# Two halves of an attention head issued in turn on different rows of the array, in a two-block kernel on one core

## The chip, the cores and the metric

The kernel runs on one core of one Trainium2 chip. The core has five engines with a queue each: TensorE (PE, its weight loads are shown as PEld), VectorE (DVE), ScalarE (ACT), GpSimd (POOL) and SyncE (SP, which here issues nearly all loads). Each of them takes its instructions in the order in which the program puts them. Matmuls write to PSUM, which has eight banks here, and everything else lives in SBUF. The metric is the device time of one execution, in microseconds.

## The reference

Two transformer blocks of width 1024 over 256 tokens, the first with 256 context tokens beside them. Only its attention matters for the change:

```python
def diff_attention(q, k_all, v_all, lam):
    ...
    def one_block(q_blk):
        s = jnp.einsum('bhcqd,bhckd->bhcqk', q_blk, k_all).astype(jnp.float32) * scale
        p = jax.nn.softmax(s, axis=-1)
        a = p[:, :, 0] - lam * p[:, :, 1]
        return jnp.einsum('bhqk,bhkd->bhqd', a.astype(v_all.dtype), v_all)
...
def first_block(x, c, ctx, ...):
    for l in range(DEPTH):                    # DEPTH = 2
        ...
        attn = diff_attn_post(diff_attention(q, k_all, v_all, lam), subln_g[l], lambda_init)
        pool_o = pool_mixer(up, pool_w[l], pool_scale[l])
        conv_o = conformer_conv(ca, cb, conv_dw_w[l], conv_dw_b[l], conv_ln_g[l], conv_ln_b[l])
        mix = jnp.concatenate([attn, pool_o, conv_o], axis=-1)
        x = x + g1 * jnp.einsum('blm,md->bld', mix, w_out[l])
        x = x + g2 * swiglu(...)
        if not last:
            ...                               # the same for the context tokens
```

There are 4 heads (h), and each has two halves (c = 0, 1) of 64 columns of q and k with one common v of 128 columns. The softmax of the second half, times lam, is taken off that of the first.

## The kernel before

All products are fp32 split in a high and a low part (`fp32r`), so that each product is three matmuls: `mm3`, lines L359 (high by high), L360 and L361. Layer 0 runs tokens and context together, 512 rows; layer 1 (the last) has only the 256 tokens as queries, against all 512 keys.

The function `attention` takes a list of units, each one a head j and a tile tt of 128 queries. In layer 0 each call has the units of one head, four calls in all: two units with 256 keys (the context tiles, which see only the context) and two with 512, 16 units altogether. In layer 1 a call has two heads of two units, two calls, 8 units, all with 512 keys. A unit is made by `scores` (two halves one after the other: three matmuls of a 64-row contraction into a bank `ps_sc`, a DVE reduce for the maximum, an ACT `Exp` into tile `e`) and by `values` (DVE joins the halves, L713; four or two transposes, L716; an ACT copy, L718; the matmuls with v, L721; an ACT square and a DVE scaling). The scores of a unit are written one unit ahead of the values of the unit before. `finish` normalizes a head once all its tiles are there (a pow on POOL, L364, and four transposes, L738).

After each unit `each()` puts other work between: eight convolution taps on DVE, some steps of the modulation's product (`fill`: eight steps to a group, each one a load `wmod` of 512 KB with two buffers and four narrow matmuls, L513, whose sums are transposed at the end, L520) and, at fixed units, `pooled(l, j, ...)` for the two groups of pooled channels. `pooled` is a projection of 512 columns (24 matmuls into a bank `ps_mm`), an ACT copy into padded tiles (L767), window sums on POOL (L772 to L781, two sequences) and a small matmul (L782) for each sequence. The conv's norm (`conv_norm`, from L828) follows with sums of one column (L437), a pow and a broadcast matmul (L452), and after it the merges of all parts with `w_out`, whose first product writes `ps_mm_2431` in layer 0.

PSUM in the first block has four pools: `mm` of three banks, `md` of one (the modulation), `sc` of two and `aux` of two. A tile waits until the bank that it gets is read out by its last user.

What sets the order: a scheduler orders the written instructions by a simulated time line of its own; each engine then has one fixed order. `tc.issue_after(P["product"].ins)` holds an instruction behind the newest product.

Of the kernel before, what the change touches and what calls it, by code (L numbers as in the profile page):

```python
# [14 lines left out]
AF = mybir.ActivationFunctionType  # L15
ALU = mybir.AluOpType
AX = mybir.AxisListType
# [260 lines left out]
def tile_two_blocks(ctx: ExitStack, tc: tile.TileContext, w: bass.AP, blk: bass.AP, cols: bass.AP,  # L278
                    rowv: bass.AP, cst: bass.AP, xin: bass.AP, out: bass.AP):
    nc = tc.nc  # L280
    dma, act, dve, pool, pe = nc.sync, nc.scalar, nc.vector, nc.gpsimd, nc.tensor

    P = {"nscr": NSCR, "both": False, "count": 0}
# [74 lines left out]
    def mm3(ps, a, b, start, stop):  # L358
        pe.matmul(ps, a[0], b[0], start=start, stop=False)  # L359
        pe.matmul(ps, a[0], b[1], start=False, stop=False)  # L360
        P["product"] = pe.matmul(ps, a[1], b[0], start=False, stop=stop)  # L361
# [4 lines left out]
    def bank(p):  # L366
        return P[p].tile([128, 512], F32, name="ps_" + p)
# [4 lines left out]
    def st(n=8):  # L372
        return P["wk"].tile([128, n], F32, name=f"st{n}", bufs=8 if n < 64 else 3)
# [313 lines left out]
    def attention(l, h0, qT, kT, v, o, qts, mix, each):  # L687

        lam, sub = coef[l][:2]
        q0 = qts[0]  # L690

        def scores(j, tt):
            nk = 256 if tt < 2 else 512
            mx, s = st(2), st(2)
            e = []
            for c in range(2):
                r = slice(c * 64, c * 64 + 64)
                ps = bank("sc")
                qs = slice((tt - q0) * 128, (tt - q0) * 128 + 128)
                mm3(ps[:, :nk], (qT[j][0][r, qs], qT[j][1][r, qs]), (kT[j][0][r, :nk], kT[j][1][r, :nk]),  # L700
                    True, True)
                dve.tensor_reduce(mx[:, c:c + 1], ps[:, :nk], axis=AX.X, op=ALU.max, negate=True)
                x = P["wk"].tile([128, 512], F32, name="e", bufs=4)
                act.activation(x[:, :nk], ps[:, :nk], AF.Exp, bias=mx[:, c:c + 1], accum_out=s[:, c:c + 1])
                e.append(x)
            return nk, s, e

        def values(j, tt, ss, nk, s, e):
            h = h0 + j
            r, cc = st(2), st(1)  # L710
            dve.reciprocal(r, s)
            dve.scalar_tensor_tensor(cc, s[:, 0:1], r[:, 1:2], lam, op0=ALU.mult, op1=ALU.mult)
            dve.scalar_tensor_tensor(e[0][:, :nk], e[1][:, :nk], cc, e[0][:, :nk], op0=ALU.mult, op1=ALU.add)  # L713
            pt = bank("aux")
            for i in range(nk // 128):
                pe.transpose(pt[:, i * 128:i * 128 + 128], e[0][:, i * 128:i * 128 + 128], ident)  # L716
            aT = P["wk"].tile([128, 512], F32, name="aT", bufs=2)
            act.copy(out=aT[:, :nk], in_=pt[:, :nk])  # L718
            po = bank("aux")
            for i in range(nk // 128):  # L720
                pe.matmul(po[:, :128], aT[:, i * 128:i * 128 + 128], v[i][:, h * 128:h * 128 + 128],  # L721
                          start=(i == 0), stop=(i == nk // 128 - 1))
            q = P["wk"].tile([128, 128], F32, name="sq128")
            i = tt - q0
            act.activation(q, po[:, :128], AF.Square, scale=r[:, 0:1], accum_out=ss[:, i:i + 1])
            dve.tensor_scalar(o[tt][:, h * 128:h * 128 + 128], po[:, :128], r[:, 0:1], None, op0=ALU.mult)

        def finish(j, ss):
            h = h0 + j
            n = len(qts)  # L730
            c = slice(h * 128, h * 128 + 128)
            dve.tensor_scalar(ss[:, :n], ss[:, :n], 1.0 / 128, EPS, op0=ALU.mult, op1=ALU.add)
            rsqrt(ss[:, :n], n)
            for i, tt in enumerate(qts):
                dve.scalar_tensor_tensor(o[tt][:, c], o[tt][:, c], ss[:, i:i + 1], sub, op0=ALU.mult, op1=ALU.mult)
            pt = bank("aux")
            for i, tt in enumerate(qts):
                pe.transpose(pt[:, i * 128:i * 128 + 128], o[tt][:, c], ident)  # L738
            m = slot()
            split(pt[:, :n * 128], m[0][:, :n * 128], m[1][:, :n * 128])  # L740
            mix[h] = m

        units = [(j, tt) for j in range(len(qT)) for tt in qts]
        sums = {j: st(4) for j in range(len(qT))}
        ahead = scores(*units[0])
        for i, (j, tt) in enumerate(units):
            now = ahead
            if i + 1 < len(units):
                ahead = scores(*units[i + 1])
            values(j, tt, sums[j], *now)  # L750
            if tt == qts[-1]:
                finish(j, sums[j])
            each()

    def pooled(l, j, h, seqs, mix):

# [101 lines left out]
    h = new_h()  # L858
# [67 lines left out]
    for l in range(DEPTH):  # L926
# [27 lines left out]
        def each():  # L954
            run_taps(8)
            if not last and unit[0] < len(FILL):
                fill(FILL[unit[0]])
            unit[0] += 1
            if jobs and unit[0] in POOL_AFTER[l]:
                jobs.pop(0)()  # L960
# [227 lines left out]
    r = st(1)  # L1188
# [483 lines left out]
```

## Time and profile before

| what | value |
|---|---|
| median of three runs | 1420.87 us (1414.85 to 1423.79) |
| the profiled execution | 1412.22 us |
| its span (first to last instruction) | 1410.4 us |
| mean granted clock of TensorE | 0.972 |
| TensorE busy | 1340.1 us, 95% |
| DVE busy | 964.5 us, 68% |
| first layer's attention, first score to the end of the last | 118.20 to 220.30 us |
| last layer's first scores | 720.10 us |

The times in views are microseconds from the start of the span. A granted clock of 1.00 is 2.4 GHz, 0.50 is 1.2 GHz. Rows of the timeline name the line of the instruction, its output tile and its inputs; equal instructions that follow each other stand in one row, with an x and their number (a matmul of fp32 type leaves two records).

### The profile page before, as it was taken

What the parts mean: (1) busy time and instruction counts of PE and PEld (TensorE: products, weight loads), DVE (VectorE), ACT (ScalarE), POOL (GpSimd) and SP (SyncE); (2) the same over time, 40 slices, a digit from 0 to 9 for tenths busy, and PEclk for the clock granted to TensorE, in tenths of its full rate; (3) what the DMA queues carried; (4) which work ended last, traced back from release to release, by engine and by line L of the source; (5) the groups of instructions that cost most, each with busy time, mean ns of one, the idle gap of its engine ahead of it and who ended that gap; (6) DMA issues with size and microseconds to landing.
All of it is one profiled execution on the core that took longest, in us unless ns stands there. A gap on an engine that the chain in (4) does not pass through costs nothing. (4 is left out here: it accounts for less than half of the span.)

```text
span 1410.4 us, 22740 instructions
## 1 busy us (share of the span) xinstructions
PE 1340.1 (95%) x8754; PEld 1172.3 (83%) x8754; DVE 964.5 (68%) x1928; ACT 602.9 (43%) x1085; POOL 233.0 (17%) x274
## 2 busy tenths in 40 slices
PE   5999999899999999998988989999999999988999
PEld 2699656798888888888977879999977889878999
DVE  4599755678666767746975755555688676757665
ACT  3333444442213222335344544444565546446443
POOL 0056630220000000014316220000263002000000
PEclk9899988999999999999988999999999999999999
DMA  9424450425445567732321235555664424424554
GB/s 342 170 78 146 156 175 30 137 90 190 160 153 167 187 217 230 240 113 75 108 87 45 95 130 177 189 180 183 191 213 149 142 84 128 150 90 152 192 184 132
DMA packets 61309, 213.53 MB, mean 151 GB/s; under 512 B 6928, under 2 KB 8080, under 8 KB 60944
## 3 DMA queue, kind: packets, MB, share of 16 engines
q1 hardware_dynamic: 60768, 209.91, 45.0%
q10 hardware_dynamic: 432, 2.16, 0.4%
q8 instruction: 69, 1.13, 0.3%
q14 instruction: 40, 0.33, 0.1%
HBM read 211.00 MB, written 1.05 MB: 150 GB/s over the span
## 5 line engine op out<-in xcount | busy, mean ns | idle before, releaser
L349 ACT CAST whi<-wraw 128x1024 fp32r<-128x1024 f32 (+2 forms) x292 | 300.5, 1033 | 528.4 <-PE ps_mm L360 271.5
L350 DVE TENSOR_TENSOR wlo<-wraw,whi 128x1024 fp32r<-128x1024 f32 (+2 forms) x296 | 356.2, 1205 | 173.0 <-ACT whi L349 168.4
L359 PE MATMUL ps_mm<-hH,whi 128*128 128x256 f32 (+1 forms) x1056 | 344.5, 329 | 11.1 <-ACT hH L497 7.5
L360 PE MATMUL ps_mm<-hL,whi 128*128 128x256 f32 (+1 forms) x1056 | 342.9, 326 | 2.5 <-DVE hL L498 2.5
L361 PE MATMUL ps_mm<-hH,wlo 128*128 128x256 f32 (+1 forms) x1056 | 342.3, 326 | 1.3 <-DVE wlo L350 1.3
L359 PEld LDWEIGHTS ps_mm<-hH,whi 128*128 128x128 f32 x1056 | 204.2, 195 | 32.9 <-ACT hH L497 9.3
L360 PEld LDWEIGHTS ps_mm<-hL,whi 128*128 128x128 f32 x1056 | 204.7, 194 | 20.0 <-DVE hL L498 4.1
L361 PEld LDWEIGHTS ps_mm<-hH,wlo 128*128 128x128 f32 x1056 | 204.6, 194 | 17.5 <-DVE wlo L350 2.3
L359 PE MATMUL ps_mm<-hidH,whi 128*128 128x256 f32 (+1 forms) x683 | 214.8, 317 | 2.6 <-ACT hidH L355 1.7
L360 PE MATMUL ps_mm<-hidL,whi 128*128 128x256 f32 (+1 forms) x683 | 214.7, 315 | 0.6 <-DVE hidL L356 0.6
L361 PE MATMUL ps_mm<-hidH,wlo 128*128 128x256 f32 (+1 forms) x683 | 213.8, 315 | 0.0
L360 PE MATMUL ps_mm<-wlo,hH 128*128 128x256 f32 (+2 forms) x464 | 143.9, 312 | 3.2 <-DVE wlo L350 3.2
L361 PE MATMUL ps_mm<-whi,hL 128*128 128x256 f32 (+2 forms) x464 | 142.6, 309 | 0.0
L359 PE MATMUL ps_mm<-whi,hH 128*128 128x256 f32 (+2 forms) x464 | 140.5, 312 | 2.1 <-ACT tm L647 1.4
L359 PEld LDWEIGHTS ps_mm<-hidH,whi 128*128 128x128 f32 x683 | 129.5, 190 | 11.9 <-ACT hidH L355 1.9
L360 PEld LDWEIGHTS ps_mm<-hidL,whi 128*128 128x128 f32 x683 | 129.9, 190 | 9.8 <-DVE hidL L356 1.2
L361 PEld LDWEIGHTS ps_mm<-hidH,wlo 128*128 128x128 f32 x683 | 129.6, 190 | 8.0
L470 POOL TENSOR_TENSOR squares<-squares,scr 128x256 f32<-128x256 f32 (+1 forms) x28 | 31.7, 1131 | 560.2 <-ACT scr L469 559.7
L580 DVE CUSTOM_DVE_ANT_0 ps_md<-wmod,tm 128x512 f32<-128x512 f32 x160 | 111.5, 697 | 10.8 <-DMA wmod<-in_w_dram 8.0
L848 DVE SCALAR_TENSOR_TENSOR xT<-ps_mm,modv,xT 128x256 f32<-128x256 f32 x116 | 52.5, 479 | 73.9 <-PE ps_mm L361 73.9
L364 POOL TENSOR_TENSOR st<-st,mhalf 128x4 f32<-128x4 f32 (+3 forms) x54 | 64.4, 1198 | 200.1 <-DVE st L632 88.1
L360 PEld LDWEIGHTS ps_mm<-wlo,hH 128*128 128x128 f32 x464 | 89.0, 192 | 9.3 <-DVE wlo L350 5.5
(347 smaller groups left out, 1987.2 us busy)
## 6 DMA issues: line engine op xcount, KB each, us to landing
wraw<-in_w_dram SPq DMA_DIRECT2D x271, 512.0 KB, 3.5
wmod<-in_w_dram SPq DMA_DIRECT2D x85, 512.0 KB, 4.2
wraw<-in_w_dram SPq DMA_DIRECT2D x32, 448.0 KB, 3.2
xT<-in_x_dram ACTq DMA_DIRECT2D x2, 1024.0 KB, 7.0
single<-in_w_dram SPq DMA_DIRECT2D x8, 256.0 KB, 7.5
wraw<-in_w_dram SPq DMA_DIRECT2D x4, 288.0 KB, 3.2
tm<-in_rows_dram SPq DMA_DIRECT2D x4, 256.0 KB, 6.1
out_dram<-scr SPq DMA_DIRECT2D x8, 128.0 KB, 1.7
```

The lines of the kernel that those rows point to most:

```text
L349: act.copy(out=hi[:, :m], in_=t[:, :m])
L350: P["split"] = dve.tensor_tensor(lo[:, :m], t[:, :m], hi[:, :m].bitcast(F32), op=ALU.subtract)
L359: pe.matmul(ps, a[0], b[0], start=start, stop=False)
L360: pe.matmul(ps, a[0], b[1], start=False, stop=False)
L361: P["product"] = pe.matmul(ps, a[1], b[0], start=False, stop=stop)
L364: pool.tensor_tensor(t, t, mhalf[:, :n], op=ALU.pow)
L470: eng.tensor_tensor(squares[:, lo:hi], squares[:, lo:hi], q, op=ALU.add)
L580: dve.tensor_tensor_reduce(bank("md"), t[:, i * 512:i * 512 + 512], crow[2 * j + i], 1.0, 0.0, ALU.mult, ALU.add, sums[j][:, i * KD + d:i ...
L848: dve.scalar_tensor_tensor(xT[:, d, r], ps[:, s * 256 - lo:s * 256 - lo + 256], M(l, which, 1 - s)[:, d:d + 1], xT[:, d, r], op0=ALU.mult, ...
```

## The change

Scores are written as six matmuls in turn, one of each half, where the second half's result goes to a bank of `mm` in place of the second bank of `sc`. Each of the six is held behind the one before. The exps are split off into a function of their own, and the first part of `values`, up to the copy of the transposes, becomes `turned`. The loop then runs scores two units ahead and `turned` one unit ahead of `values`; exps of a unit come after the `turned` of the unit two before it.

```diff
         def scores(j, tt):
             nk = 256 if tt < 2 else 512
             mx, s = st(2), st(2)
+            ps = [bank("sc"), bank("mm")]
+            qs = slice((tt - q0) * 128, (tt - q0) * 128 + 128)
+            for i, (a, b) in enumerate(((0, 0), (0, 1), (1, 0))):
+                for c in range(2):
+                    r = slice(c * 64, c * 64 + 64)
+                    with tc.issue_after(P["product"].ins) if i or c else nullcontext():
+                        P["product"] = pe.matmul(ps[c][:, :nk], qT[j][a][r, qs], kT[j][b][r, :nk], start=i == 0,
+                                                 stop=i == 2)
+            for c in range(2):
+                dve.tensor_reduce(mx[:, c:c + 1], ps[c][:, :nk], axis=AX.X, op=ALU.max, negate=True)
+            return nk, ps, mx, s
+
+        def exps(nk, ps, mx, s):
             e = []
             for c in range(2):
-                r = slice(c * 64, c * 64 + 64)
-                ps = bank("sc")
...
-                mm3(ps[:, :nk], (qT[j][0][r, qs], qT[j][1][r, qs]), (kT[j][0][r, :nk], kT[j][1][r, :nk]),
-                    True, True)
-                dve.tensor_reduce(mx[:, c:c + 1], ps[:, :nk], axis=AX.X, op=ALU.max, negate=True)
                 x = P["wk"].tile([128, 512], F32, name="e", bufs=4)
-                act.activation(x[:, :nk], ps[:, :nk], AF.Exp, bias=mx[:, c:c + 1], accum_out=s[:, c:c + 1])
+                act.activation(x[:, :nk], ps[c][:, :nk], AF.Exp, bias=mx[:, c:c + 1], accum_out=s[:, c:c + 1])
...
-        def values(j, tt, ss, nk, s, e):
-            h = h0 + j
+        def turned(j, tt, nk, s, e):
...
             act.copy(out=aT[:, :nk], in_=pt[:, :nk])
+            return nk, r, aT
+
+        def values(j, tt, ss, nk, r, aT):
+            h = h0 + j
             po = bank("aux")
...
-        ahead = scores(*units[0])
-        for i, (j, tt) in enumerate(units):
-            now = ahead
-            if i + 1 < len(units):
-                ahead = scores(*units[i + 1])
-            values(j, tt, sums[j], *now)
-            if tt == qts[-1]:
-                finish(j, sums[j])
-            each()
+        n = len(units)
+        held = {i: exps(*scores(*units[i])) for i in range(min(2, n))}
+        turn = {}
+        for i in range(n + 1):
+            ahead = scores(*units[i + 2]) if i + 2 < n else None
+            if i:
+                j, tt = units[i - 1]
+                values(j, tt, sums[j], *turn.pop(i - 1))
+                if tt == qts[-1]:
+                    finish(j, sums[j])
+            if i < n:
+                turn[i] = turned(*units[i], *held.pop(i))
+                if ahead:
+                    held[i + 2] = exps(*ahead)
+                each()
```

The text grows by 18 lines, so that later lines have other numbers after (L772 becomes L790, L782 L800). In the new order all score matmuls have the one line L702.

TensorE early in layer 0's attention, before: the scores of the first head's second unit and what follows them (`ps_sc` are the scores, `ps_md` the modulation, `ps_mm` a projection).

```order
L359 MATMUL ps_sc_1285<-hidH_670,hidH_661 128x256
L360 MATMUL ps_sc_1285<-hidL_671,hidH_661 128x256
L361 MATMUL ps_sc_1285<-hidH_670,hidL_662 128x256
L359 MATMUL ps_sc_1292<-hidH_670,hidH_661 128x256
L360 MATMUL ps_sc_1292<-hidL_671,hidH_661 128x256
L361 MATMUL ps_sc_1292<-hidH_670,hidL_662 128x256
L513 MATMUL ps_md_1323<-wmod_1324,csil_109 32x256 x4
```

The same place after:

```order
L702 MATMUL ps_mm_1286<-hidH_670,hidH_661 128x256
L702 MATMUL ps_sc_1285<-hidL_671,hidH_661 128x256
L702 MATMUL ps_mm_1286<-hidL_671,hidH_661 128x256
L702 MATMUL ps_sc_1285<-hidH_670,hidL_662 128x256
L702 MATMUL ps_mm_1286<-hidH_670,hidL_662 128x256
L702 MATMUL ps_sc_1301<-hidH_670,hidH_661 128x512
L702 MATMUL ps_mm_1302<-hidH_670,hidH_661 128x512
L702 MATMUL ps_sc_1301<-hidL_671,hidH_661 128x512
```

The halves take turns, and the next unit (512 keys) follows at once.

TensorE at the end of layer 0's attention, after: the last scores, and what comes behind them (`ps_mm_2211` is the first pooled projection, whose products stood, before, between the scores of the first and the second head; the second one, `ps_mm_2289`, and all small pooled matmuls come later still).

```order
L702 MATMUL ps_sc_2173<-hidH_1672,hidL_1664 128x512
L702 MATMUL ps_mm_2174<-hidH_1672,hidL_1664 128x512
L520 MATMUL ps_md_1965<-first_75,cp_2084 128x128 x2
L733 MATMUL ps_aux_2089<-tm_682,aT_2070 128x128
L733 MATMUL ps_aux_2089<-tm_683,aT_2070 128x128
L733 MATMUL ps_aux_2089<-tm_684,aT_2070 128x128
L733 MATMUL ps_aux_2089<-tm_685,aT_2070 128x128
L359 MATMUL ps_mm_2211<-hH_157,whi_2207 128x512
```

What moved is the pooled projection, from among the scores to behind the last of them.

POOL in the same stretch, before: the last rope (L658), the rope tables for layer 1 (L620, L618) with the window sums (L772 to L781) between, and then the first head's pow, `st4_1266`.

```order
L658 TENSOR_TENSOR tm_979<-tm_979,own_457 128x256
L620 TENSOR_TENSOR other_5895<-cstt_440,rowt_441 128x2x32
L772 TENSOR_TENSOR scr_2233<-scr_2193 128x271
L620 TENSOR_TENSOR other_5895<-cstt_440,rowt_441 128x2x32 x3
L618 TENSOR_TENSOR own_5894<-cstt_440,rowt_441 128x2x64 x2
L773 TENSOR_TENSOR scr_2234<-scr_2233 128x269
L779 TENSOR_TENSOR scr_2234<-scr_2233,cstt_440 64x256
L780 TENSOR_TENSOR scr_2234<-scr_2234,cstt_440 64x256
L772 TENSOR_TENSOR scr_2241<-scr_2194 128x271
L781 TENSOR_TENSOR scr_2234<-scr_2234,scr_2193 128x256
L773 TENSOR_TENSOR scr_2242<-scr_2241 128x269
L364 TENSOR_TENSOR st4_1266<-st4_1266,mhalf_79 128x4
```

After:

```order
L658 TENSOR_TENSOR tm_979<-tm_979,own_457 128x256
L620 TENSOR_TENSOR other_5895<-cstt_440,rowt_441 128x2x32 x4
L364 TENSOR_TENSOR st4_1266<-st4_1266,mhalf_79 128x4
L618 TENSOR_TENSOR own_5894<-cstt_440,rowt_441 128x2x64 x2
L364 TENSOR_TENSOR st4_1676<-st4_1676,mhalf_79 128x4
L364 TENSOR_TENSOR st4_1906<-st4_1906,mhalf_79 128x4
L790 TENSOR_TENSOR scr_2243<-scr_2203 128x271
L791 TENSOR_TENSOR scr_2244<-scr_2243 128x269
```

The window sums now come behind the pows of the first three heads.

DVE in layer 1, just before its first scores are read, before: the last taps (L820), weight splits (L350), the low parts of k and q (`hidL`, L356) and the first maxima (L702).

```order
L350 TENSOR_TENSOR wlo_6821<-wraw_6818,whi_6820 128x1024
L820 SCALAR_TENSOR_TENSOR cacc_6030<-cu_5877,colt_70,cacc_6030 128x256 x2
L659 TENSOR_TENSOR tm_6034<-tm_6034,scr_6289 128x256
L350 TENSOR_TENSOR wlo_6916<-wraw_6913,whi_6915 128x1024
L820 SCALAR_TENSOR_TENSOR cacc_6030<-cu_5877,colt_70,cacc_6030 128x256 x3
L350 TENSOR_TENSOR wlo_6922<-wraw_6919,whi_6921 128x1024
L356 TENSOR_TENSOR hidL_6298<-ps_aux_6294,hidH_6297 128x256
L356 TENSOR_TENSOR hidL_6305<-ps_aux_6301,hidH_6304 128x256
```

After:

```order
L838 SCALAR_TENSOR_TENSOR cacc_6030<-cu_5877,colt_70,cacc_6030 128x256 x6
L659 TENSOR_TENSOR tm_6034<-tm_6034,scr_6289 128x256
L838 SCALAR_TENSOR_TENSOR cacc_6030<-cu_5877,colt_70,cacc_6030 128x256 x2
L356 TENSOR_TENSOR hidL_6298<-ps_aux_6294,hidH_6297 128x256
L838 SCALAR_TENSOR_TENSOR cacc_6030<-cu_5877,colt_70,cacc_6030 128x256
L356 TENSOR_TENSOR hidL_6305<-ps_aux_6301,hidH_6304 128x256
L705 TENSOR_REDUCE st2_6438<-ps_sc_6440 128x1
L705 TENSOR_REDUCE st2_6438<-ps_mm_6441 128x1
```

The three weight splits have gone behind the maxima. On TensorE the first scores of layer 1 (`ps_sc_6440`, `ps_mm_6441`) stand 147 rows earlier than before, ahead of the projections of the next two heads (`ps_mm_6652` and on) and not behind them.

## Rows read from the trace of the kernel before

**Rows 1.** The page: busy time of each engine and share of the span.
```profile
PE 1340.1 (95%) x8754; PEld 1172.3 (83%) x8754; DVE 964.5 (68%) x1928; ACT 602.9 (43%) x1085; POOL 233.0 (17%) x274
```
**Rows 2.** Timeline of TensorE: start us, us, engine, line, operation, out<-in, count.
```profile
127.39 0.39 PE L359 MATMUL ps_sc<-hidH 64*128 64x256 f32 x2
...
127.95 0.64 PE L513 MATMUL ps_md<-wmod,csil 128*32 128x256 f32 x8
...
134.02 0.49 PE L359 MATMUL ps_sc<-hidH 64*128 64x512 f32 x1
...
134.91 0.38 PE L359 MATMUL ps_mm<-whi,hH 128*128 128x256 f32 x1
...
156.38 0.38 PE L359 MATMUL ps_sc<-hidH 64*128 64x256 f32 x1
...
156.93 0.64 PE L513 MATMUL ps_md<-wmod,csil 128*32 128x256 f32 x8
```
**Rows 3.** Windows: busy us of PE, PEld, DVE, ACT, POOL; clock, DMA share, GB/s.
```profile
118.20:220.30 102.10, 99.72 (x671) 69.68 (x670) 73.58 (x166) 46.77 (x135) 49.35 (x71) 0.93 0.45 153
199.50:213.10 13.60, 13.60 (x71) 7.70 (x67) 5.56 (x15) 5.26 (x17) 0.00 (x0) 0.50 0.35 116
```
**Rows 4.** Timeline of TensorE in layer 0's attention.
```profile
160.38 1.16 PE L721 MATMUL ps_aux<-tm,aT 128*128 128x128 f32 x8
161.37 0.60 PE L716 MATMUL ps_aux<-first,e 128*128 128x128 f32 x4
...
171.82 0.39 PE L359 MATMUL ps_mm<-hH,whi 128*128 128x512 f32 x1
172.05 0.39 PE L360 MATMUL ps_mm<-hL,whi 128*128 128x512 f32 x1
...
189.40 0.70 PE L782 MATMUL ps_mm<-scr,colt 128*128 128x256 f32 x2
189.93 1.88 PE L828 MATMUL ps_mm<-cacc,ones 128*128 128x512 f32 x4
...
196.30 1.40 PE L437 MATMUL ps_mm<-ones,scr 128*128 128x1 f32 x12
...
226.12 1.42 PE L359 MATMUL ps_mm<-hidH,whi 128*128 128x512 f32 x1
```
**Rows 5.** Tile wmod, 118 to 215 us: idle time of its queue, landing time.
```profile
  DMA wmod<-in_w_dram: 4.4, 7
...
DMA to landing us min/median/max: 3.1/3.4/5.5
```
**Rows 6.** Timelines of ACT and POOL, second pooled group.
```profile
178.08 1.04 ACT L349 CAST whi<-wraw 128x1024 fp32r<-128x1024 f32 x1 [1.84 <-PE ps_mm L360]
...
179.54 1.34 POOL L772 TENSOR_TENSOR scr<-scr 128x271 f32<-128x271 f32 x1 [8.65 <-ACT scr L767]
...
190.86 0.72 POOL L781 TENSOR_TENSOR scr<-scr 128x256 f32<-128x256 f32 x1
```
**Rows 7.** Timelines of ACT and POOL, conv norm of layer 0.
```profile
192.57 1.29 ACT L834 ACTIVATE scr<-cacc 128x512 f32<-128x512 f32 x2 [1.98 <-DVE cacc L831]
...
222.48 1.50 POOL L364 TENSOR_TENSOR st<-st,mhalf 128x4 f32<-128x4 f32 x1 [2.26 <-DVE st L441]
```
**Rows 8.** Timelines of TensorE and DVE at layer 1's scores.
```profile
719.62 1.23 DVE L350 TENSOR_TENSOR wlo<-wraw,whi 128x1024 fp32r<-128x1024 f32 x1 [0.49 <-ACT whi L349]
...
720.10 0.50 PE L359 MATMUL ps_sc<-hidH 64*128 64x512 f32 x2
...
720.77 0.75 DVE L356 TENSOR_TENSOR hidL<-ps_aux,hidH 128x256 fp32r<-128x256 f32 x2
...
721.24 0.50 PE L361 MATMUL ps_sc<-hidH,hidL 64*128 64x512 f32 x2 [0.40 <-DVE hidL L356]
...
724.11 0.49 PE L359 MATMUL ps_sc<-hidH 64*128 64x512 f32 x1 [2.37 <-ACT e L704]
...
762.79 0.80 PE L359 MATMUL ps_sc<-hidH 64*128 64x512 f32 x2 [0.46 <-ACT hidH L355]
```

More of the change, by code (lines that the diff above doesn't have):

```diff
@@ L694, in scores @@
             mx, s = st(2), st(2)
+            ps = [bank("sc"), bank("mm")]
[10 more added lines that the diff above has]
+        def exps(nk, ps, mx, s):
             e = []
             for c in range(2):
-                r = slice(c * 64, c * 64 + 64)
-                ps = bank("sc")
-                qs = slice((tt - q0) * 128, (tt - q0) * 128 + 128)
-                mm3(ps[:, :nk], (qT[j][0][r, qs], qT[j][1][r, qs]), (kT[j][0][r, :nk], kT[j][1][r, :nk]),
-                    True, True)
-                dve.tensor_reduce(mx[:, c:c + 1], ps[:, :nk], axis=AX.X, op=ALU.max, negate=True)
                 x = P["wk"].tile([128, 512], F32, name="e", bufs=4)
-                act.activation(x[:, :nk], ps[:, :nk], AF.Exp, bias=mx[:, c:c + 1], accum_out=s[:, c:c + 1])
+                act.activation(x[:, :nk], ps[c][:, :nk], AF.Exp, bias=mx[:, c:c + 1], accum_out=s[:, c:c + 1])
                 e.append(x)
             return nk, s, e
-        def values(j, tt, ss, nk, s, e):
-            h = h0 + j
+        def turned(j, tt, nk, s, e):
             r, cc = st(2), st(1)
```

## The prediction

> **What bounds the kernel now.** The first lines of the page come first [rows 1]: TensorE is busy 95% of the span of 1410.4 us and no other engine reaches 70%, so the average says "TensorE bound". The run behind that page took 1412.22 us, 1.8 us more than its span, and the sum below is made against it; the median of the three runs is 1420.87 us, 0.6% higher, and the answer is carried over to that. The average hides that the attention stages are limited by what TensorE waits for, so the second view is TensorE's timeline inside them [rows 2]. What to see there are two distances. At 127.39 us the two halves of a head start together (one row, x2) and the next work starts at 127.95: 0.56 us for both halves. At 156.38 a half stands alone and the next work starts 0.55 us later; with 512 keys one half alone takes 134.91 − 134.02 = 0.89. So a pair costs what a half costs, and the pair of 127.39 was in program order three products of one half, then three of the other: the old order already overlaps whenever nothing stands between. What can be won is only the halves that other work separates. Third come the windows of the first layer's attention [rows 3]: from the first score to the end of the last it takes 102.1 us, TensorE is busy 99.7 of them, and in 13.6 of them the granted clock was 0.50, the lower level of 1.2 GHz.
>
> **The halves.** In the first layer 6 of the 8 units with 256 keys and all 8 with 512 are split up in the old order: 6 × 0.55 + 8 × 0.89 = 10.4 us. In the last layer 6 of 8 units are, all of 512 keys: 5.3. That is 15.7 us, 1.1%, if nothing else moved.
>
> In those rows the later half started ahead of the earlier half's second product [rows 2]. The Trainium skill, page "TensorE: Matmul & The Clock Gate", Part 3, says that matmuls start and end strictly in program order; by it the old order could not overlap at all, all 24 units would gain, and this term would be 8 × 0.55 + 16 × 0.89 = 18.6. The row disagrees, and the sum keeps 15.7.
>
> **What the second bank moves, layer 0.** The second half's scores now sit in a bank of "mm", the three banks that the projections use too. The order shows the price: the two 512-wide projections of the pooled branch, which stood between the scores, are now behind the last score, and with them the POOL chain that they feed, its four matmuls, the conv's mean and its norm. Until there the middle gets shorter, by
> - 10.4 for the halves;
> - 24 matmuls of 0.22 (172.05 − 171.82, rounded) for each projection, 10.6 [rows 4];
> - four pooled matmuls of 0.53 (189.93 − 189.40) 2.1, the conv's sums 1.9, its one-column sums 2.0 (1.40 for twelve of sixteen records, with 0.6 for the rest): 6.0 [rows 4];
> - one unit's values and a modulation transpose, 1.3 (values of a 512-key unit are 161.37 − 160.38 = 0.99 [rows 4]).
> So 102.1 − 28.3 = 73.8, and the last score would end at 118.2 + 73.8 = 192.0. In this packed middle the 16 modulation steps come faster than the loads behind them: two "wmod" buffers, and the queue already idled on them for 4.4 us in 7 places, with a median landing of 3.4 us [rows 5]. A pair of steps needs a new load each about 3.9 us (landing plus issue); laid along the new order that gives 9.0 us of waits. The clock loss of 13.6 us at half rate is 6.8 us and follows idle stretches too, so I count half of the waits as lying on it: 4.5. Last score ends: 196.5.
>
> After it nothing is left to hide the chain behind, in order:
> - rest of the attention ahead of the first projection 1.3, the projection 5.3;
> - cast and pads on ACT, then POOL's first result for head group 0: the cast is 1.04 [rows 6], the pads 0.6 (an estimate: half its elements), six POOL operations 4.3 (0.72 each [rows 6]), a matmul 0.5: 6.4, and TensorE has only transposes and values to fill it;
> - the second projection 5.3: it stands behind the first pooled matmul in the order, so it cannot move up;
> - cast and pads again 1.6, then POOL's two sequences of group 1, from 179.54 to 190.86 + 0.72, so 12.0 [rows 6], with a pow of up to 1.50 [rows 7] that may stand between: 15.1;
> - the last pooled matmul 0.5, the conv's sums 1.9 behind it, the two squares 1.3 [rows 7], the one-column sums under 1.0; from pow to merges it took 226.12 − 222.48 = 3.6 before [rows 4, 7]; less 0.4 that overlaps: 7.9.
> Sum 41.6; the merges start at 238.1. Before they started at 226.12 [rows 4], with some 4.3 us of unfinished attention (three units of values and transposes, 1.5 each) still inside, so 230.4 is the number to compare: **+7.7 us**. The tail, 41.6 against 10.1 before (230.4 − 220.3), eats the 23.8 us that the middle gives (220.3 − 196.5) and more, because work of TensorE that was filler becomes a chain of ACT, POOL and TensorE in turn.
>
> The Trainium skill, page "TensorEngine Tiling (Array Packing)", section Gotcha 1, says that row tiles write to different PSUM banks and so raise PSUM pressure, which speaks against this change. The order bears the pressure out, not as a slower matmul but as a delay of others; without it the sum would be the 15.7 us of gain alone.
>
> **Layer 1.** Before, 144 projection matmuls of the next heads ran ahead of the first scores and hid the wait for the rope of q; scores started at 720.10 and then waited 0.40 and 2.37 for DVE and ACT [rows 8]. Now the first scores stand ahead of those projections, which need the banks that the scores hold. A product of 256 columns takes half of the 0.23 of 512 [rows 4], so TensorE is free 144 × 0.12 = 17.3 and some transposes (1.4) earlier, at 701.4, but the score's last operand, hidL, was written at 721.5 by DVE [rows 8]; three weight splits of 1.23 us, less what their overlap hides (3.4 together) leave DVE's queue ahead of it and a gap of 0.5 closes: 717.4. So TensorE idles some 16 us. Four units then pass through two banks of "sc", three waits for exps of the 2.37 us seen there before [rows 8], and the projections go on at about 724.5; 240 × 0.12 = 28.8, four units' values (0.99 [rows 4]) and transposes at 1.6 together, and 1 us for the rest carry to 760.9. After 16 idle us a clock loss like the 6.8 us at half rate that the old trace has in other places costs 3.4: 764.3 against 762.79 [rows 8], and 1.7 for the rope of the next pair: **+3**. The rest of that layer's order is as before. The 5.3 us of halves are inside this sum.
>
> **Queues.** SP's queue keeps the order of its loads; the "wmod" loads come earlier and wait for buffers, and the raw weights queued behind them are the next merges', not needed before 230. On ACT, exps of units two ahead now stand in front of the copies for transposes: no cost, since those have a unit more of time.
>
> **Rivals.**
> 1. *Forecast: waits take the place of what is saved*, +10.7 on the sum, median 1431.5; its range is +5 to +19 (load waits wholly on the path 4.5 more, clock loss in the second half of the middle 4 more; or up to 6 us of the tail's idle time filled).
> 2. *The clock stays at its lower level through the new middle and the tail.* For it: the new middle waits for loads 16 times and 13.6 us at 0.50 arose in the old one with fewer [rows 3, 5]. It decides if the lower level stands for some 30 us more than in the sum, the second half of the middle and the TensorE work of the tail: half of them, 15, on top of 10.7. That is +19 to +32 around +26, median 1447. Against it: the 0.93 of the whole old middle is used up by that one stretch (6.8 of 102.1 us) [rows 3].
> 3. *Faster: the look-ahead pays.* The queues of ACT and POOL run the tail in parallel with the unfinished units, loads land in time (no waits, −9 with the clock loss), and layer 1's idle time hides under a DVE chain that ends earlier. It decides in layer 0 when the tail is under 33.9 us (10.1 + 23.8). At 28 it gives −5.9, without the load waits −4.5 more, and in layer 1 the halves' −5.3: −15.7 in all, median 1405. Against it: the second projection behind the first pooled matmul is fixed by the order, as is POOL's 12.0 us.
> 4. *It does not do what it says*: the halves were no loss, because TensorE then waits for the softmax in their place, and some 8 us of the tail are filled with units that the look-ahead left over, so that layer 0 comes out even; layer 1's halves pay its wait: −3 to +5, median 1422.
>
> **How the numbers follow.** Chances 0.55, 0.15, 0.12, 0.18. The time is the likeliest case's: 1420.87 + 10.7 = 1431.5. The range leaves out most of case 3 and the upper part of case 2: 1417 to 1447. A change of 1%, 14 us, is about what the measurement can tell from none: the three runs spread over 0.6%. Faster by over 1%: half of case 3, 0.06. Slower by over 1% (above 1435): case 2 with 0.15, and of case 1 the upper two fifths, 0.21: 0.36. The rest, 0.58, is within 1%.
>
> **What would show it.** In the changed profile: the pairs start as one row (x2) everywhere, the last score of layer 0 ends near 197, a stretch of about 40 us with a TensorE below half busy stands between it and the merges at about 238, with POOL as releaser; in layer 1 a wait of 10 to 18 us for DVE's hidL stands ahead of the scores at about 717, and projections end near 761 to 765. If the last score ends near 197 and the merges begin before 228, case 3 holds; if the granted clock is 0.5 for 30 us and more in the middle, case 2. The forecast is wrong if the scores wait for "mm" banks, which I have priced at nothing beyond the order, or if POOL's chain starts before the last score.

## The result, and the profile after

The changed kernel takes 1435.17 us (median of 4 runs, 1428.15 to 1437.83) against 1417.86 of the kernel before (4 runs): 1.013 times as long, 95% interval 1.0092 to 1.0168, some 18 us (17.3 between the two medians). The forecast was 1431.5, in a range of 1417 to 1447. The profiled execution of it is the fastest of the four, 1428.15 us with a span of 1426.3.

The page of the changed kernel, its span and its first part, which answers to [rows 1]:

```profile
span 1426.3 us, 22753 instructions
...
PE 1324.6 (93%) x8754; PEld 1165.3 (82%) x8754; DVE 963.2 (68%) x1928; ACT 603.4 (42%) x1085; POOL 235.8 (17%) x274
```

TensorE is busy 15.5 us less than before and the span is 15.9 us longer: the saving of busy time that the change is about is there, and 31 us of idle time have come with it. To see where, two stages are cut at products that both kernels have: the first from a projection ahead of layer 0's attention into the merges behind it, the second from a product ahead of layer 1's attention (L452) into the merges behind that. Windows of the kernel before (columns as in [rows 3]):

```profile
60.70:262.30 201.60, 196.35 (x1297) 156.56 (x1298) 155.98 (x307) 87.27 (x208) 77.62 (x93) 0.95 0.34 115
658.20:793.70 135.50, 121.30 (x834) 108.68 (x832) 105.39 (x226) 66.49 (x144) 53.43 (x67) 0.91 0.21 71
```

and of the changed kernel, with its window behind the last scores of layer 0:

```profile
57.30:268.80 211.50, 187.14 (x1297) 151.88 (x1297) 154.72 (x307) 87.39 (x208) 77.09 (x94) 0.94 0.33 110
664.60:807.80 143.20, 113.19 (x830) 103.59 (x829) 106.03 (x225) 66.62 (x145) 54.65 (x65) 0.88 0.20 67
...
200.00:240.00 40.00, 27.30 (x98) 19.20 (x99) 15.78 (x26) 12.33 (x30) 20.25 (x30) 0.70 0.08 27
```

Layer 0's stage is 9.9 us longer and layer 1's 7.7. What is left over is small: the start was 3.4 us shorter in this execution, and what comes behind layer 1's stage, which the change doesn't touch, is 1.8 longer (618.5 in place of 616.7). In both stages TensorE's busy time went down (by 9.2 and 8.1 us) and its idle time up (from 5.3 to 24.4 us, and from 14.2 to 30.0). The last window is the tail of layer 0: DMA at 8%, POOL busy for half of it, TensorE's granted clock at 0.70.

The timeline of TensorE in layer 0 of the changed kernel, the last scores, the two pooled projections (first products) and the end:

```profile
191.29 0.50 PE L702 MATMUL ps_sc<-hidH 64*128 64x512 f32 x1
191.29 0.49 PE L702 MATMUL ps_mm<-hidH 64*128 64x512 f32 x1
...
192.18 0.44 PE L520 MATMUL ps_md<-first,cp 128*128 128x128 f32 x2
192.46 1.06 PE L733 MATMUL ps_aux<-tm,aT 128*128 128x128 f32 x8
193.27 0.48 PE L359 MATMUL ps_mm<-hH,whi 128*128 128x512 f32 x1
...
206.42 0.99 PE L359 MATMUL ps_mm<-hH,whi 128*128 128x512 f32 x1
...
221.81 0.47 PE L750 MATMUL ps_aux<-first,tm 128*128 128x128 f32 x1 [4.30 <-DVE tm L747]
...
236.11 2.08 PE L452 MATMUL ps_mm<-scr,ones 128*128 128x512 f32 x2 [2.08 <-DVE scr L448]
237.20 1.42 PE L359 MATMUL ps_mm<-hidH,whi 128*128 128x512 f32 x1
```

Both halves start at once (191.29) and are done 0.89 us later, what one half alone took before [rows 2]. From the end of the scores, 192.2, to the merges, 237.2, it takes 45.0 us. POOL in that stretch, first and last window sum of each pooled group:

```profile
200.21 1.41 POOL L790 TENSOR_TENSOR scr<-scr 128x271 f32<-128x271 f32 x1 [4.35 <-ACT scr L785]
...
208.17 0.64 POOL L799 TENSOR_TENSOR scr<-scr 128x256 f32<-128x256 f32 x1
214.76 1.34 POOL L790 TENSOR_TENSOR scr<-scr 128x271 f32<-128x271 f32 x1 [5.94 <-ACT scr L785]
...
226.23 0.72 POOL L799 TENSOR_TENSOR scr<-scr 128x256 f32<-128x256 f32 x1
```

The second group's chain ran from 179.54 to 191.58 before, under the scores [rows 6], and runs from 214.76 to 226.95 now; TensorE was busy for 10.8 of those 12.0 us and is for 6.1 of 12.2 now.

Layer 1, waits of TensorE from 664 to 813 us (us in total, times, longest), and its timeline at the last unit of the stage:

```profile
PE ps_aux L671 <- DVE tm L659: 16.9, 4, 7.0
PE ps_aux L750 <- DVE tm L747: 4.6, 1, 4.6
PE ps_sc L702 <- ACT e L712: 2.7, 3, 1.2
PE ps_mm L800 <- POOL scr L799: 2.7, 1, 2.7
```
```profile
773.78 0.49 PE L702 MATMUL ps_sc<-hidH 64*128 64x512 f32 x1
774.20 0.66 PE L724 MATMUL ps_aux<-first,e 128*128 128x128 f32 x4
775.70 1.16 PE L733 MATMUL ps_aux<-tm,aT 128*128 128x128 f32 x8 [0.84 <-ACT aT L726]
779.54 1.22 PE L800 MATMUL ps_mm<-scr,colt 128*128 128x256 f32 x2 [2.69 <-POOL scr L799]
780.70 0.79 PE L702 MATMUL ps_mm<-hidH 64*128 64x512 f32 x1
```

Of the 16.9 us, 15.5 are idle time ahead of the first scores (three waits of 4.1, 7.0 and 4.4 for DVE's last step of the rope, L659), which start at 721.29 (720.10 before [rows 8]); the fourth, of 1.4, is ahead of the next pair of heads. Layer 1's stage starts 6.4 us later in this profile (664.6 in place of 658.2), so the first scores come 5.2 us earlier in it than before. The timeline shows something that the prediction had not: the first half of the last unit starts at 773.78 and its partner 6.9 us later. Ahead of the partner in TensorE's queue stands the first pooled group's small matmul (L800), which waits for POOL until 779.54; the bank that comes to the partner in mm's line is that of the unit before, whose exp ends at 776.2. The second pooled projection, which ran from 765.94 before, stands behind the partner and starts at 782.27. Its first product, the last window sum on POOL and the first merge, before:

```profile
765.94 0.78 PE L359 MATMUL ps_mm<-hH,whi 128*128 128x256 f32 x1
...
779.99 0.73 POOL L781 TENSOR_TENSOR scr<-scr 128x256 f32<-128x256 f32 x1
...
789.07 0.47 PE L359 MATMUL ps_mm<-hidH,whi 128*128 128x256 f32 x1
```

and after:

```profile
782.27 0.58 PE L359 MATMUL ps_mm<-hH,whi 128*128 128x256 f32 x1
...
794.27 0.73 POOL L799 TENSOR_TENSOR scr<-scr 128x256 f32<-128x256 f32 x1
...
803.05 0.47 PE L359 MATMUL ps_mm<-hidH,whi 128*128 128x256 f32 x1
```

### The profile page after: what moved, and what is told of

Read it like the earlier page. It is cut to its first block, busy times and chain, and to the rows that moved or that the text cites. A ratio compares the mean times of both kernels' runs of the same rounds, so it can differ in the third digit from the quotient of the medians.

```text
span 1426.3 us, 22753 instructions
## 1 busy us (share of the span) xinstructions
PE 1324.6 (93%) x8754; PEld 1165.3 (82%) x8754; DVE 963.2 (68%) x1928; ACT 603.4 (42%) x1085; POOL 235.8 (17%) x274
## 5 line engine op out<-in xcount | busy, mean ns | idle before, releaser
L350 DVE TENSOR_TENSOR wlo<-wraw,whi 128x1024 fp32r<-128x1024 f32 (+2 forms) x296 | 356.6, 1207 | 178.9 <-ACT whi L349 173.9
L364 POOL TENSOR_TENSOR st<-st,mhalf 128x4 f32<-128x4 f32 (+3 forms) x54 | 68.7, 1277 | 178.3 <-DVE st L632 83.6
```

What stands on the lines that cost most here:

```text
L350: P["split"] = dve.tensor_tensor(lo[:, :m], t[:, :m], hi[:, :m].bitcast(F32), op=ALU.subtract)
L364: pool.tensor_tensor(t, t, mhalf[:, :n], op=ALU.pow)
```

## The experiments

Three things change at once: the second half's bank, the issue in turn, and the look-ahead. **Theory A** (the banks) says that the text's order of mm tiles ties the pooled work to the scores. **Theory B** puts the loss on the look-ahead or the issue. Later a **theory C** was added: layer 1's old order was a fortunate one, which any change ahead of it spoils. All times are ratios to the kernel before, measured beside it, with the 95% interval. The attention stages are given as "layer 0's stage" and "layer 1's stage", cut as above (201.6 and 135.5 us before, 211.5 and 143.2 after).

**e1: both halves in sc.** In the changed kernel:

```diff
-            ps = [bank("sc"), bank("mm")]
+            ps = [bank("sc"), bank("sc")]
```

> The changed kernel, with both halves of a unit in the two banks of sc and none in mm. Theory A (the banks): the loss comes from the second half's use of mm, whose banks go round in the order of the text, so that the pooled projections, written at units 14 and 15 and at 5 and 6, end up behind the last scores. Then the projections are back among the scores, layer 0's merges start at 224 to 231 us in place of 237, layer 1's at 785 to 792 in place of 803, and the time is 0.985 to 1.003 of the kernel before. Theory B (the look-ahead and the order of issue): the loss comes from scores two units ahead, which bring exps, loads and waits closer together. Then it stays at 1.008 to 1.018 with the projections moved back.

Measured 1.0146 (1.0106 to 1.0187), stages 208.5 and 147.5 us. Layer 0's merges did come back, to 229.6, but layer 1's start at 806.6, and the time is no better, in the range of theory B. Theory A in its simple form falls: without the bank the look-ahead costs as much.

**e2: three by three.** The two loops of the six matmuls exchanged, `for c` outside.

> The changed kernel with the six score matmuls written as three of one half, then three of the other, instead of in turn; banks and look-ahead as changed. If adjacent halves overlap in the array however they are written (as the old row at 127.39 us), the pairs still start as one and the time is that of the changed kernel, 1.009 to 1.017 of the one before. If the turn is what makes them overlap, each pair costs 0.5 to 0.9 us more, 18 us in all, 1.022 to 1.03.

Measured 1.0135 (1.0095 to 1.0175), as the changed kernel. The timeline of TensorE early in layer 0:

```profile
125.84 0.38 PE L702 MATMUL ps_mm<-hidH 64*128 64x256 f32 x1
125.86 0.49 PE L702 MATMUL ps_sc<-hidH 64*128 64x512 f32 x1
126.07 0.28 PE L702 MATMUL ps_mm<-hidL,hidH 64*128 64x256 f32 x1
126.19 0.28 PE L702 MATMUL ps_mm<-hidH,hidL 64*128 64x256 f32 x1
```

The second row is the next unit's first half. In the program it stands behind all three products of the half in rows 1, 3 and 4, and it starts 0.02 us after the first. Work on the other rows of the array is taken ahead, so issue in turn is not what makes halves overlap; standing next to each other is. It also means that the sentence ahead of the prediction, by which each engine takes its instructions in the program's order, is not exact for TensorE. (The Trainium skill, page "TensorE: Matmul & The Clock Gate", Part 3, says that matmuls start strictly in program order; this row disagrees with it, as the one at 127.39 did. By that rule the last product of one half could still overlap the first of the other, so the prediction's 18.6 is too high even by the page.)

What the turn does is to keep the halves next to each other. Not all pairs start as one in e2: the last unit of layer 1 has its halves at 781.67 and 789.70, and the scores of that layer keep TensorE busy for 14.4 us, 10.9 in the changed kernel. The time doesn't show it: 1.0135 and 1.0130.

**e3: the bank alone.** In the kernel before:

```diff
-                ps = bank("sc")
+                ps = bank("sc" if c == 0 else "mm")
```

> The kernel before with one change: the second half's scores go to a bank of mm. Order of issue, look-ahead and the rest are the old ones. Theory A: the pooled projections move behind the scores here too; layer 0's merges start at 235 to 245 us, layer 1 ends 5 to 12 us later, 1.008 to 1.025. Theory B: nothing of the loss, 0.997 to 1.004.

Measured 1.0211 (1.0175 to 1.0247), stages 224.7 and 148.1 us, layer 0's merges at 252. One word costs 2.1%, more than the whole change. That is in theory A's range; the merges come later than its 245. In layer 0 the second pooled chain begins only at 230.58:

```profile
230.58 1.34 POOL L772 TENSOR_TENSOR scr<-scr 128x271 f32<-128x271 f32 x1 [10.59 <-ACT scr L767]
```

**e4: the turn alone.** In the kernel before, six matmuls in turn as in the change, but into two banks of sc, one unit ahead.

> The kernel before with one change: the two halves are issued in turn into the two banks of sc; scores one unit ahead as before. Theory A: a small gain from the halves that other work had separated (15.7 us at most, less the waits of TensorE for the softmax, which now gates both halves at once): 0.990 to 1.002. Theory B, in the form that pairs wait for both banks: 1.003 to 1.01.

Measured 0.9989 (0.9962 to 1.0015): no difference, in theory A's range.

**e5: the whole change in layer 0 only; e6 and e7: the turn of e4 in layer 0 only, and in layer 1 only.** Both versions of `attention` stand side by side:

```diff
+    def attention(l, *args):
+        (attention_last if l else attention_first)(l, *args)
```

> The whole change in layer 0 only; layer 1 keeps the old attention. The traces put the loss of the changed kernel at about 9 us in layer 0 and 9 in layer 1. Theory A (in layer 0 the mm banks move the pooled chain behind the scores; in layer 1 the loss has a cause of its own): 1.004 to 1.010, layer 0's merges at 235 to 239 us. Theory C (layer 1's old order comes back only by chance, and any change ahead of it costs there too): 1.011 or more.

> Halves issued in turn into the two sc banks, scores one unit ahead, in layer 0 only; layer 1 as before. In the run with both layers so, layer 0's merges came 10 us earlier and layer 1 gave 12 back. Theory A: 0.990 to 0.996. Theory C: 0.997 to 1.004.

> The same in layer 1 only; layer 0 as before. Theory A: layer 1 loses some 10 us from the pairs themselves (both halves wait for both banks' exps), 1.004 to 1.010. Theory C: the loss of layer 1 came with the changes ahead of it; then the 5 us of halves are saved or nothing, 0.996 to 1.002.

Measured 1.0133 (1.0088 to 1.0178), 0.9973 (0.9945 to 1.0001) and 1.004 (1.0012 to 1.0067). e5 is above what theory A had and as theory C has it, e6 too is in theory C's range, and e7 is in theory A's and above theory C's. In e7's layer 1 the scores wait for exps for 7.4 us in 7 places, 2.9 in 2 before: pairs that need both banks at once do wait longer there. The profiled execution of e5 has stages of 217.6 and 140.0 us; the first has the changed kernel's order, which took 211.5 there. Layer 1 with the old text took 4.5 us longer than before, and its order on the engines did change. e7 gave the most useful windows, since its layer 0 is instruction for instruction the old one. Windows of e7 and of e4, both stages:

```profile
57.40:253.80 196.40, 191.79 (x1298) 154.18 (x1298) 155.79 (x307) 87.41 (x208) 77.50 (x93) 0.97 0.35 119
651.20:790.00 138.80, 119.60 (x832) 107.32 (x831) 105.39 (x225) 66.25 (x144) 53.30 (x67) 0.90 0.21 69
```
```profile
58.30:253.40 195.10, 184.70 (x1297) 150.87 (x1298) 153.57 (x307) 87.51 (x208) 78.46 (x93) 0.97 0.35 119
650.70:793.70 143.00, 122.13 (x828) 107.69 (x827) 106.01 (x225) 66.42 (x143) 55.14 (x65) 0.86 0.20 67
```

At the same clock, 0.97, the turn takes 7.1 us off TensorE's busy time in layer 0 (191.79 to 184.70), and the stage gets 1.3 us shorter: 5.8 us are waits that were work before. The waits of TensorE in layer 0 (118 to 222 us) name them. e7, then e4:

```profile
PE ps_md L513 <- DMA wmod<-in_w_dram: 1.4, 3, 0.9
...
PE ps_sc L359 <- ACT e L704: 0.8, 2, 0.4
```
```profile
PE ps_md L513 <- DMA wmod<-in_w_dram: 5.5, 6, 1.7
PE ps_sc L702 <- ACT e L707: 2.4, 2, 1.4
```

The loads and the exps have become the later ones: 4.1 and 1.6 us more.

**e8: e5 with the pooled jobs early in layer 0.**

```diff
-POOL_AFTER = ((14, 15), (5, 6))
+POOL_AFTER = ((4, 6), (5, 6))
```

> As the first of this call (the whole change in layer 0 only), and the two pooled jobs of layer 0 written at units 4 and 6 in place of 14 and 15, so that their banks' turn comes among the scores. Theory A: the POOL chain is done before the last score, the merges start at 212 to 222 us, 0.986 to 0.996. If instead the look-ahead or the loads are what costs in layer 0, the merges stay behind 226: 1.000 to 1.008.

Measured 1.0055 (1.003 to 1.0081), 0.8% under e5; layer 0's merges at 227 in place of 245, its stage 203.8 in place of 217.6. By the expectation's own marks this is its second case: the merges stay behind 226, and the time is in 1.000 to 1.008. So moving the pooled work takes back some 0.8% of the 1.3%, as theory A has it in kind, and the rest of layer 0's loss has another cause. TensorE waits 8.0 us for `wmod` loads in this stage (1.5 before) and 3.4 for exps (0.8 before); but e4 has 5.5 us of load waits without a loss, so that these waits alone don't settle it.

**e9: the changed kernel with pooled jobs early in both layers**, `((4, 6), (1, 2))`.

> The whole change in both layers, with the pooled jobs written early in both: at units 4 and 6 of layer 0 and 1 and 2 of layer 1, in place of 14 and 15 and of 5 and 6. Theory A says that in both layers the pooled projections and the POOL chain, held behind the scores by the mm banks, make the loss; in layer 0 alone this gave back 0.8%. Then 0.997 to 1.005. If layer 1 loses by the rope's chain ahead of its first scores instead, the pooled job moved there does not help: 1.006 to 1.012.

Measured 1.0145 (1.0113 to 1.0178), above both ranges, stages 204.8 and 155.3. Layer 0 is as in e8, but layer 1 is 12 us longer than after the change; the early place is worse there, and the 16.9 us for the rope are still there (18.2). Theory A's remedy fails in layer 1.

**e10: the bank and the turn**, e4 with `ps = [bank("sc"), bank("mm")]`.

> The kernel before with the halves issued in turn and the second half in a bank of mm; scores one unit ahead and values in one piece, as before. The bank alone cost 2.1%, the turn alone 0 and the whole change costs 1.3%. If the look-ahead is what takes 0.8% back, this stays at 1.017 to 1.024; if the turn takes it back, 1.010 to 1.016.

Measured 1.0143 (1.0112 to 1.0175), stages 217.7 and 143.9. So with the bank of mm the turn takes 0.7% of its 2.1% back (by the intervals, 0.2 to 1.2), and the look-ahead nothing that can be measured.

**e11: e6 with early pooled jobs**, `((4, 6), (5, 6))`.

> In search of a faster one: halves in turn into the two sc banks in layer 0 alone (0.9973 when measured so), and layer 0's pooled jobs written at units 4 and 6. With two sc banks the pooled chain was already hidden, so moving it should change nothing: 0.994 to 1.000. If its early place frees the end of the stage, 0.988 to 0.993.

Measured 1.0049 (1.0024 to 1.0074), above both ranges, layer 0's stage 208.0 against 196.8 in e6. The same move that gains 0.8% between e5 and e8 costs 0.8% here: with banks of sc the late place was the good one. Why early costs there stays open.

**e12: e1 with the scores of two units ahead written behind the transposes.**

```diff
-            ahead = scores(*units[i + 2]) if i + 2 < n else None
...
-                if ahead:
-                    held[i + 2] = exps(*ahead)
+                if i + 2 < n:
+                    held[i + 2] = exps(*scores(*units[i + 2]))
```

> As the run with both halves in sc and scores two units ahead (1.0146), but the scores of the unit two ahead are written behind the transposes of the current unit, not ahead of the values of the one before. Theory D: with two banks the scores two ahead stand in TensorE's queue waiting for exps, with values and transposes queued behind them, and that is the 1.5%; then 0.997 to 1.005. If it is not their place in the queue, 1.010 to 1.018 again.

Measured 0.9998 (0.9978 to 1.0018), stages 198.0 and 139.0: theory D holds. What the queue looked like in e1, TensorE's timeline in layer 1:

```profile
728.87 1.46 PE L702 MATMUL ps_sc<-hidH 64*128 64x512 f32 x2 [1.59 <-ACT e L712]
...
732.36 1.46 PE L702 MATMUL ps_sc<-hidH 64*128 64x512 f32 x2 [1.18 <-ACT e L712]
...
736.73 1.09 PE L724 MATMUL ps_aux<-first,e 128*128 128x128 f32 x4 [2.06 <-DVE e L721]
```

Pair after pair waits for the exps that free its two banks; the first transposes come only behind three of them and then wait for DVE's part of the softmax. The waits of TensorE in layer 1 (664 to 813 us), of e1 and then of e12:

```profile
PE ps_sc L702 <- ACT e L712: 5.0, 4, 2.0
PE ps_aux L724 <- DVE e L721: 4.9, 2, 2.8
PE ps_aux L724 <- DVE st L719: 3.4, 2, 2.0
```
```profile
PE ps_sc L702 <- ACT e L712: 7.7, 6, 3.2
...
PE ps_aux L724 <- DVE e L721: 0.2, 1, 0.2
```

The scores wait for exps in both, and no less in e12; what has gone are the waits of the transposes, 8.3 us in e1 and 0.2 in e12. Of the 8.5 us by which layer 1's stage is shorter, 5.3 are idle time of TensorE and 3.2 busy time, at a granted clock of 0.90 in place of 0.85. Layer 0's is 10.5 shorter, 7.1 of it busy time (0.97 in place of 0.94), so that there the cause is less plain.

## Why the prediction was right, and where it was off

**The side and the size** were forecast: +10.7 us against some 18 (1.3%), inside the range, and by the mechanism of case 1: the bank of mm costs (e3), the turn alone doesn't (e4), and bank and turn without the look-ahead cost what the whole change does (e10). The nearness of 1431.5 to 1435.17 is in part luck: both layers cost more than their terms (+9.9 against +7.7 and +7.7 against +3 in the profiles), and the kernel before came out at 1417.86 in place of 1420.87. Three of its additions are also a little off: the tail's terms make 41.3 and not 41.6, and in layer 1 the steps to 717.4 and 760.9 make 717.6 and 760.7.

**The halves.** That the pairs overlap when adjacent, and that the old order did so too, was right (e2). (In layer 0 the trace of before has three units of 256 keys with adjacent halves, at 118.16, 127.39 and 211.32, so 5 of 8 were split and not 6, which is 0.55 us less.) That 10.4 and 5.3 us would be saved as time was not: alone, the turn saves 7.1 us of busy time in layer 0 and no time that can be measured (0.9989 in e4, 0.9973 in e6; in layer 1 alone it costs, 1.004 in e7). Of the sum this term is mis-sized. What took its place in layer 0 is for 4.1 us the loads, which the sum had as a term of its own, and for 1.6 us the exps, which is rival 4's reason.

**Layer 0's middle and tail.** The stage started 3.4 us earlier in the changed profile, so 3.4 is added here to its times. The last score was forecast to end at 196.5 and ended at 195.6; the tail was forecast at 41.6 and took 45.0; the merges were forecast at 238.1 and started at 240.6. In the tail TensorE was busy for 32.0 of the 45.0 us, not below half, and its longest wait has DVE as releaser, behind a pow of POOL (219.98 to 221.00) that stands among the window sums. e5 has the same 45.0 us (199.9 to 244.9 of its span). That the bank of mm is what moves the pooled work behind the scores is shown from both sides: the bank alone brings the delay (e3: merges at 252), and jobs written earlier take a good part of it away (e8: merges at 227 in place of e5's 245, 0.8% of the 1.3%). The load waits were forecast at 9.0 us, half of them on the path; the changed kernel shows 5.0 in 7 places. That the clock's loss follows idle stretches is not what the old trace shows at that place: the clock fell at 199.5 after 9.5 us (190.0 to 199.5) in which TensorE was busy throughout at 1.00. The stage came out at +9.9 in this pair of profiles against +7.7. The size is soft: e7 shows the old layer 0 in 196.4 us where the profile of before has 201.6, and e5, with the changed layer 0, has 217.6, so that the true figure may be nearer to 15. The time of e5 says 19 us for the change in layer 0 alone, with an interval of 12 to 25.

**Layer 1.** Up to the second pair of heads the mechanism holds: idle time of 16 us forecast, 15.5 shown. That the bank brings it is shown by the other runs: the waits for L659, 16.9 us in all here, are 16.4 to 18.2 in e2, e3, e9 and e10, which have scores of layer 1 in mm, and at most 0.7 in the kernel before and in the other runs, which have them all in sc. Its releaser is the rope, and not hidL. Less the 6.4 us by which the stage starts later, projections go on at 721.2 (724.5 forecast) and the next scores come at 759.3 (764.3 and 1.7 for the rope forecast, 762.79 before): 3.5 us gained up to here, where +3 was forecast. The step that failed is "the rest of that layer's order is as before": from there to the merges it took 26.3 us before and takes 37.3 now (765.73 to 803.05), 11.0 more. It is layer 0's mechanism over again, a second pooled projection that stands behind the last scores, here with a partner half 6.9 us late ahead of it, and a POOL chain that ends at 795.0 in place of 780.7 (788.6 when the 6.4 us are taken off). It was worked out for one layer and not looked for in the other. The whole of layer 1 is +7.7 against the forecast +3.

**What stays open.** Layer 1 with the old text is 2 to 4.5 us longer in e5 and e6 than before (140.0 and 137.5 against 135.5), as the scheduler gives it another order when something ahead changes. The order looks like the reason: e11 has the old order of that layer again and takes 134.6, and e8, with nearly the order of e5, 139.2. Four profiles don't prove it. So e5 (layer 0 alone, 1.0133) and the whole change (1.0130) can't be taken apart to give layer 1 a price by timing; its price rests on the traces. What costs layer 0 the rest when the pooled work is early (e8) is open too. No version beats the old kernel for certain: e6, at 0.9973, ends at 1.0001.

**Rivals.** The clock (case 2) did not last: 0.94 over the stage, though 0.76 in the tail (192.2 to 237.2). At two levels, 0.94 of 211.5 us stands for some 25 us at the lower one, 0.95 of 201.6 for some 20; the case asked for 30 more. (e5's 0.91 of 217.6 stands for some 39, 19 more than before.) The look-ahead (case 3) pays nothing: with the mm bank it changes 1.0143 to 1.0130, with sc banks it costs 1.5% as long as it stands ahead in the queue (e1, e12).

## What to carry to other kernels

A tile that is moved to another pool joins that pool's line: ask what else takes its turn there, where in the text it is written, and which chain of other engines hangs on it; one bank moved cost 2.1% here, with the same matmuls. Busy time taken off the busiest engine is time saved only where nothing else is due at once: read the next wait first (here the loads of 512 KB and the exps). Work issued ahead must find its buffers free, or it holds up what stands behind it in the queue (e1, e12); and a mechanism found in one layer is to be looked for in each of the others.

## What the runs showed of the hardware

One and the same stream of instructions takes different times in one stage: layer 0 of the kernel before took 201.6 us in its profile and 196.4 in e7's, with the same order on DVE, ACT and POOL; 4.6 of the 5.2 us are busy time of TensorE, and most of that is the granted clock. In the kernel before it was at 0.50 for 13.6 us (199.5 to 213.1, [rows 3]); in e7 the drop at this place and the stretch behind it were

```profile
196.60:200.40 3.80, 3.80 (x21) 2.04 (x19) 1.73 (x4) 1.39 (x4) 0.00 (x0) 0.55 0.42 138
...
200.40:217.00 16.60, 14.78 (x94) 9.48 (x92) 12.38 (x35) 11.13 (x36) 2.51 (x2) 0.90 0.19 63
```

Over the whole stage a clock of 0.95 in 201.6 us and of 0.97 in 196.4 lose 10.1 and 5.9 us, 4.2 of the 5.2. Single profiles of this kernel can't tell stages apart to better than that.

The other thing is what the row at 127.39 had shown and e2 shows again, across two units: products on different rows of the array start within 0.02 us of each other even when three products of one stand ahead of the other's first in the program.
